# The low part of each query sub-head in a tile of its own, over zeros, in a two-layer diffusion block

## The chip, the core and the metric

The kernel runs on one core of a Trainium2 chip. The metric is the device time of one execution in microseconds (us); three runs of the kernel before took 2702.43, 2704.64 and 2705.81 us, median 2704.64 us. One further execution was profiled, and all rows below are from it. The engines are named as in the profile: PE is the tensor engine's matmul, PEld its weight load, DVE the vector engine, ACT the scalar engine, POOL the GpSimd engine, SP the engine that issues the DMAs.

## The reference

Two layers of a transformer block over 256 context tokens and 512 latent tokens (T = 768), 1024 features wide. A normed and modulated input is projected to four branches: softmax attention A (the differential attention below), attention B (eight heads over latent projections), a pooling mixer and a convolution mixer. They are merged with sigmoid gates, projected, and followed by a squared-relu MLP. Attention A, which the change touches, in the reference's own words:

```
def attend(qs, ks, v, coef):          # qs: (2 sub-heads, batch, 4 heads, tokens, 64)
    ...
        sc = jnp.einsum('mbhqd,mbhkd->mbhqk', qi, ks, preferred_element_type=jnp.float32) * scale
        p = jnp.einsum('m,mbhqk->bhqk', coef, jax.nn.softmax(sc, axis=-1))
        return jnp.einsum('bhqk,bhkd->bhqd', p.astype(v.dtype), v)
```

Each of the four heads has two sub-heads of 64 features; each sub-head has its own scores and its own softmax, and the second is subtracted from the first with a learned weight. In the first layer the 256 context queries see the 256 context keys and the 512 latent queries see all 768 keys; in the second layer only the latent queries are computed.

## The kernel before

All products run in the float32r format. To keep float32 accuracy a value is split into a high part (rounded to float32r by an ACT copy) and a low part (the rest, by a DVE subtraction), and a product is made of high x high, high x low and low x high.

For the scores of attention A the splitting is packed. A sub-head has 64 features, a tile 128 partitions. `a_qk` projects the queries (or keys) of two heads, norms and rotates them token-major, transposes them on the PE into PSUM (`pst`) and writes, for sub-head j of head hd:

- keys: one tile `ks0` or `ks1`, with the high part on the sub-head's own 64 partitions (`me`) and the low part on the other 64 (`other`);
- queries: one tile `qd0` or `qd1`, with the high part on `me` and a full copy of the value on `other`, so that one product over 128 partitions gives high x high plus (value) x low;
- queries, low part: one tile `ql` for both sub-heads, sub-head 0 on partitions 0 to 63 and sub-head 1 on 64 to 127.

`scores` makes a score tile of 128 queries by up to 768 keys in one PSUM buffer (`sc`; its pool has a single buffer): first `qd` x `ks` over 128 partitions, then `ql` x `ks` over the 64 partitions of the sub-head, accumulated. Keys are taken in chunks of 512 and 256 columns, so a tile with 768 keys is four matmuls and one with 256 keys is two. `softmax_exp` takes the maximum on DVE (`st`) and the exponential on ACT (`e`); `a_attn` combines the two sub-heads' tiles, transposes and splits them (`ph`, `pl`), and multiplies with the values `va`. Attention B does the same with 96-feature heads, with separate tiles for high and low (`bqh`, `bql`, `bkh`, `bkl`), always over 96 partitions.

The order of the work is not the order in which the code is written. Every instruction is recorded into streams (B: projections, A: attention, F: filler such as gate, pooling and convolution products, M: modulation vectors); `Plan.order` then gives each a key and lays them out with a model of the engines, and `replay` emits them in that order. Each engine runs its instructions in order. Every instruction is thus recorded at one line, L352, and the profile is read by tiles.

Tiles `ks`, `qd`, `ql`, `va`, `b..`, the split weights `wgh`/`wgl` of the latent projections and the MLP's `ah`/`al` share pool `g`, with 24 buffers of 128 x 768; a new tile waits until a buffer's former tile has been read for the last time. POOL has almost nothing to do: it clears the padding of the pooling and convolution buffers (`pool`, `cu`).

Of the kernel before, what the change touches and what calls it, by code (L numbers as in the profile page):

```python
# [20 lines left out]
# packed per-layer column constants  # L21
C_BM, C_G1, C_G2, C_SP, C_WC, C_GCQ, C_GCKV, C_GS, NCOL = 0, 48, 56, 64, 68, 80, 83, 85, 86
# packed per-layer row constants
# [4 lines left out]
# gate tiles made beside the attention, and the share of that filler at each of its steps, per layer  # L28
# [11 lines left out]
class _Rec:  # L40
    """Stands for an engine while the program is recorded."""
# [10 lines left out]
class Plan:  # L52
    """Orders the recorded instructions over the engines.

    The program is recorded as streams that run side by side within a phase. Every instruction gets a key (how far
    its stream has come, in tensor engine time); a model of the engines then issues, on each engine, the ready
    instruction with the least key. Slots of a pool tag are given out in recorded order."""
# [4 lines left out]
    def __init__(self):  # L62
        self.ops = []        # (eng, fn, meth, args, kw, key)
        self.keys = []
        self.hold = {}       # op -> earliest time
        self.phase = []
        self.nphase = 0
        self.phase_ops = {}
        self.base = 0.0
        self.stream = 'B'  # L70
        self.pe = 0.0
        self.mode = 'ff'

    # ---- recording
# [14 lines left out]
    def flush(self, span=None, lead=None):  # L89
        """ends a phase: streams are spread evenly over the time of the tensor engine in it"""  # L90
        tot = {s: sum(self.ops[i][4] for i in o if self.ops[i][0] == 'PE') for s, o in self.phase_ops.items()}
        all_ = sum(tot.values())
        for s, o in self.phase_ops.items():
            t = 0.0
            eng = 'DVE' if s == 'M' else 'PE'
            f = all_ / max(sum(self.ops[i][4] for i in o if self.ops[i][0] == eng), 1.0)
            off, sc = (lead or {}).get(s, (0.0, 1.0))
            for i in o:
                self.keys[i] = self.base + off * all_ + sc * t * f
                if self.ops[i][0] == eng:  # L100
                    t += self.ops[i][4]
        if HOLD:
            for i in self.phase_ops.get('M', ()):
                if self.ops[i][0] == 'SP':
                    self.hold[i] = self.keys[i] * HOLD
        self.base += all_
        self.phase_ops = {}
        self.nphase += 1
        self.stream = 'B'
# [52 lines left out]
    # ---- ordering  # L162
    def order(self):
# [4 lines left out]
        tiles = {}      # name -> [tag, bufs, first op, number of ops]  # L168
# [40 lines left out]
        # slots  # L209
        tagq, tagfree, first = {}, {}, {}  # L210
        unmet = {}      # tag -> phase -> tiles without a slot yet
# [28 lines left out]
        def try_slots(i):  # L240
            """gives op i the slots of the tiles that it is first to touch, or leaves it waiting"""
            while first.get(i):
                nm_ = first[i][-1]
                tag = tiles[nm_][0]
                if tag.split('_')[0] in self.DYN:
                    ph = self.phase[i]
                    if not tagfree[tag] or any(p < ph for p in unmet[tag]):
                        heapq.heappush(waiting.setdefault(tag, []), (ph, self.keys[i], i))
                        return False
                    t = heapq.heappop(tagfree[tag])  # L250
                    ready_t[i] = max(ready_t[i], t)
                    first[i].pop()
                    unmet[tag][ph] -= 1
                    if not unmet[tag][ph]:
                        del unmet[tag][ph]
                        if tagfree[tag] and waiting.get(tag):
                            wake.append(heapq.heappop(waiting[tag])[2])
                    continue
                q = tagq[tag]
                if q[-1][1] != nm_ or not tagfree[tag]:  # L260
                    return False
                t = heapq.heappop(tagfree[tag])
                ready_t[i] = max(ready_t[i], t)
                q.pop()
                first[i].pop()
                if q and tagfree[tag]:
                    wake.append(q[-1][0])
            return True
# [95 lines left out]
def tile_block(ctx, tc, xT, ccol, wmod, cols, rows, wqkv, wcq, wckv, wuq, wukv, wpool,  # L364
# [61 lines left out]
    def wset():  # L426
        """a weight slot: filler has its own; phases of dense products alone use both sets in turn"""
        if plan.mode != 'attn':
            wturn[0] += 1
            return (wfp, "wf") if wturn[0] % 2 == 0 else (wbp, "wb")  # L430
        return (wfp, "wf") if plan.stream == 'F' else (wbp, "wb")
# [28 lines left out]
    def rsqrt(ss, n, scale):  # L460
        """[128, n] of rsqrt(ss * scale + eps); scale is a float or a list of (lo, hi, scale)."""
# [11 lines left out]
    # ---------------------------------------------------------------- constants  # L473
# [5 lines left out]
    # cosines of all token tiles and sines of the x tiles (context has no rotation), times the gains  # L479
# [13 lines left out]
    # ---------------------------------------------------------------- modulation vectors  # L493
    # silu of c and c_ctx, features on partitions: [128, kt, vector]
# [14 lines left out]
    def mod_half_pe(hf, between=lambda kt: None):  # L509
        """shift and scale of the first norm for half of the features, on the tensor engine"""  # L510
# [19 lines left out]
    def mod_chunk(l, ch):  # L530
        """one chunk of the modulation vectors, products and sums over the feature tiles on the vector
        engine; yields between the feature tiles"""
# [43 lines left out]
    # ---------------------------------------------------------------- feature-major helpers  # L576
# [23 lines left out]
    def norm_r(ss, a, b):  # L600
        """1 / rms of the tokens a..b, on all partitions"""
# [16 lines left out]
    def norm_scale(l, c_g, m0, v, d0, d1):  # L618
        """g * (1 + scale) of the features"""
        ab = st(16)  # L620
        V.scalar_tensor_tensor(out=ab[:, d0:d1], in0=mods[l][:, 8 * (m0 + 1) + d0:8 * (m0 + 1) + d1, v], scalar=1.0,
                               in1=col(l, c_g + d0, d1 - d0), op0=ALU.add, op1=ALU.mult)
        return ab
# [4 lines left out]
    def norm_apply(l, x_t, R, ab, m0, seg, res, d0=0, d1=8, alt=False):  # L628
        """modulate(rmsnorm(x), mod[m0], mod[m0+1]) of a segment as split tiles"""
# [11 lines left out]
    # ---------------------------------------------------------------- layer tables  # L641
# [26 lines left out]
    # ---------------------------------------------------------------- token-major projections  # L668
    def tokmm(ps, off, n, h, w, tt, passes_w):
        """ps[:, off:off+n] = h[tokens tt]^T @ W; w(kt) -> (hi, lo) rhs."""  # L670
        nk = len(h)
        sl = slice(tt * 128, tt * 128 + 128)
        for kt in range(nk):
            hh, hl = h[kt]
            wh, wl = w(kt)
            for i, (a, b) in enumerate(((hh, wh), (hh, wl), (hl, wh))):
                PE.matmul(ps[:, off:off + n], lhsT=a[:, sl], rhs=b, start=(kt == 0 and i == 0),
                          stop=(kt == nk - 1 and i == 2))
# [11 lines left out]
    def a_qk(l, h1, hp, isk, hook):  # L690
        w = ahead.pop() if ahead else chunk_w(l, (2 if isk else 0) + hp)
        res = [tuple(g_tile(n=x) for x in (("ks0", "ks1") if isk else ("qd0", "qd1", "ql"))) for _ in range(2)]
        for tl in halves(l == DEPTH - 1 and not isk):
# [31 lines left out]
            for hd in range(2):  # L725
# [4 lines left out]
                for j in range(2):  # L730
# [5 lines left out]
                    else:  # L736
# [4 lines left out]
                        V.tensor_tensor(out=res[hd][2][me, c], in0=pt[me, :], in1=x[me, c], op=ALU.subtract)  # L741
# [19 lines left out]
    def scores(terms, t, nk):  # L761
        """q tile t with the keys; terms: (q, k, partitions)"""
# [14 lines left out]
    def a_attn(l, q, k, v, head, ydr):  # L777
# [4 lines left out]
        for t in range(t0, 6):  # L782
# [3 lines left out]
            for j in range(2):  # L786
                ps = scores(((q[j], k[j], slice(0, 128)), (q[2], k[j], slice(64 * j, 64 * j + 64))), t, nk)
# [46 lines left out]
    def rope_b_apply(dst, u, n, g, tab, t0, rbuf):  # L834
        """dst, u: [128, n, g, 32] views; tables rows t0.."""
# [11 lines left out]
    def b_latent(l, h1, hook):  # L847
        last = l == DEPTH - 1
        # q latent
# [28 lines left out]
        # kv latent and shared rotary key  # L878
# [147 lines left out]
    # ---------------------------------------------------------------- pool and conv mixers  # L1026
# [4 lines left out]
    def pad_segs(full, a, b):  # L1031
        """(psum/token slice, padded offset) of the segments."""
# [59 lines left out]
    def conv_branch(l, h1, i, ydr):  # L1092
        """yields after each of its three projections"""
# [51 lines left out]
    # ---------------------------------------------------------------- the layers  # L1145
# [27 lines left out]
    for l in range(DEPTH):  # L1173
# [30 lines left out]
        def do_fill():  # L1204
            """emit filler in proportion to the other work of the phase"""
# [11 lines left out]
        # attention inputs and attention  # L1217
# [29 lines left out]
        # gates, branch projections, merge  # L1247
# [45 lines left out]
        # output projection and residual  # L1293
# [10 lines left out]
        def step():  # L1304
            """one feature tile of a norm goes between the products of the other part"""
# [3 lines left out]
        def wkeep(key, src, pi):  # L1309
            """the split weights of a unit; the last units of the first part are used again by the second"""  # L1310
# [23 lines left out]
        # squared-relu MLP  # L1334
# [68 lines left out]
def _prep(i):  # L1403
    """Layouts of the inputs and constants that depend on shapes alone."""
# [77 lines left out]
```

## Time and profile before

| what | value |
|---|---|
| runs of the kernel | 2702.43, 2704.64, 2705.81 us; median 2704.64 us |
| profiled execution: span from the first to the last instruction | 2700.7 us (the page gives no time of it beside the span; the median lies 3.9 us above the span) |
| PE matmul busy | 2671.3 us, 99% of the span, 15620 matmuls |
| PE weight load busy | 2311.1 us, 86% |
| DVE busy | 1753.5 us, 65% |
| ACT busy | 1170.3 us, 43% |
| POOL busy | 3.3 us, 47 instructions |
| granted PE clock, mean | 0.999 of full speed |

The busy time of a matmul in the profile reaches past the moment at which the next one starts, because matmuls are pipelined. What a matmul costs the PE is therefore read from the distance between one start and the next, and these distances stand in the timeline rows.

### The profile page before, as it was taken

Reading aid. Unit: us, or ns where it says so; the run is one execution under the profiler, and the core shown is the slowest. Engines: PE = TensorE matmul, PEld = TensorE weight load, DVE = VectorE, ACT = ScalarE, POOL = GpSimd, SP = SyncE. Lnnn points to the kernel's source line nnn. Section 1 sums busy time; section 2 is a strip of 40 time slices with the busy share of each in tenths; the row PEclk is TensorE's granted clock in tenths of the full one; section 3 lists DMA queues with packets and bytes.
Section 4 is the critical chain, followed back from the end, with each engine's and each line's share of the span. In section 5 each row is a group of like instructions: output and inputs, shape, how many; then the busy total and the mean of one; then the engine's idle time right before and its main releaser. Section 6 shows DMA issues by size and latency. Waiting matters only on the chain.

```text
span 2700.7 us, 41931 instructions
## 1 busy us (share of the span) xinstructions
PE 2671.3 (99%) x15620; PEld 2311.1 (86%) x15620; DVE 1753.5 (65%) x3978; ACT 1170.3 (43%) x2444; POOL 3.3 (0%) x47
## 2 busy tenths in 40 slices
PE   8999999999999999999999999999999999999999
PEld 4888889989998888988888888887888887998887
DVE  6668666689987777445455477776467887743333
ACT  4445443446555235414141444554455562544332
POOL 0000000000000000000000000000000000000000
PEclk9999999999999999999999999999999999999999
DMA  7211223334336743333444422223332366433322
GB/s 243 77 54 58 88 91 116 104 119 129 114 122 203 226 143 104 102 96 107 125 129 129 129 90 85 72 65 99 97 104 71 93 196 213 143 116 94 101 94 78
DMA packets 189533, 311.90 MB, mean 115 GB/s; under 512 B 21520, under 2 KB 72080, under 8 KB 189328
## 3 DMA queue, kind: packets, MB, share of 16 engines
q1 hardware_dynamic: 189328, 309.22, 36.9%
q8 instruction: 123, 2.02, 0.3%
q14 instruction: 82, 0.67, 0.1%
HBM read 270.86 MB, written 38.27 MB: 114 GB/s over the span
## 4 chain that ended last, share of the span: by engine, by line
PE 94%; DMA 2%; DVE 2%; ACT 1%; issue 0%; SPq 0%; ACTq 0%; DVEq 0%
PE mm L352 80%; PE pst L352 8%; PE sc L352 5%; DMA wmp<-in_wmod_dram 1%; DMA tmp<-y 1%; DVE wl L352 0%; ACT wh L352 0%; DMA wr<-in_wff_dram 0%; DMA wr<-in_wqkv_dram 0%; DVE hl L352 0%; DVE e L352 0%; DVE qd L352 0%; PE R L352 0%; DMA gt<-g 0%; DMA y<-yt 0%
## 5 line engine op out<-in xcount | busy, mean ns | idle before, releaser
L352 ACT ACTIVATE wh<-wr 128x512 fp32r<-128x512 f32 (+2 forms) x664 | 396.1, 617 | 738.7 <-PE mm L352 621.6
L352 PE MATMUL mm<-hh,wh 128*128 128x256 f32 (+1 forms) x1984 | 614.7, 354 | 2.2 <-DVE xx L352 1.0
L352 PE MATMUL mm<-hh,wl 128*128 128x256 f32 (+1 forms) x1984 | 613.3, 354 | 0.6 <-DVE wl L352 0.6
L352 PE MATMUL mm<-hl,wh 128*128 128x256 f32 (+1 forms) x1984 | 611.0, 354 | 0.0
L352 DVE TENSOR_TENSOR wl<-wr,wh 128x512 fp32r<-128x512 f32 (+2 forms) x664 | 440.7, 674 | 219.2 <-ACT wh L352 211.1
L352 PEld LDWEIGHTS mm<-hh,wh 128*128 128x128 f32 x1984 | 370.5, 189 | 50.6 <-issue 4.6
L352 PEld LDWEIGHTS mm<-hh,wl 128*128 128x128 f32 x1984 | 371.3, 189 | 49.3 <-issue 3.5
L352 PEld LDWEIGHTS mm<-hl,wh 128*128 128x128 f32 x1984 | 370.8, 189 | 47.7 <-issue 3.0
L352 DVE SCALAR_TENSOR_TENSOR macc<-wm,silu,macc 128x256 f32<-128x256 f32 x448 | 205.2, 479 | 97.5 <-DMA wm<-in_wmod_dram 92.5
L352 PE MATMUL mm<-ah,wh 128*128 128x512 f32 (+1 forms) x768 | 242.0, 355 | 0.4 <-ACT wh L352 0.3
L352 PE MATMUL mm<-al,wh 128*128 128x512 f32 (+1 forms) x768 | 241.8, 355 | 0.0
L352 PE MATMUL mm<-ah,wl 128*128 128x512 f32 (+1 forms) x768 | 241.1, 355 | 0.0
L352 DVE SCALAR_TENSOR_TENSOR xx<-mm,mod,xx 128x256 f32<-128x256 f32 (+1 forms) x96 | 61.3, 659 | 170.2 <-PE mm L352 170.2
L352 ACT ACTIVATE ph<-pst 128x384 fp32r<-128x384 f32 (+1 forms) x216 | 102.9, 477 | 151.6 <-PE pst L352 150.8
L352 PEld LDWEIGHTS mm<-ah,wh 128*128 128x128 f32 x768 | 144.6, 188 | 21.7 <-ACT wh L352 0.8
L352 PEld LDWEIGHTS mm<-al,wh 128*128 128x128 f32 x768 | 144.5, 188 | 20.9 <-issue 0.2
L352 PEld LDWEIGHTS mm<-ah,wl 128*128 128x128 f32 x768 | 144.4, 188 | 20.8 <-issue 0.2
L352 ACT ACTIVATE e<-sc,st 128x768 f32<-128x768 f32 (+1 forms) x160 | 130.2, 814 | 73.5 <-DVE st L352 50.6
L352 PE MATMUL mm<-wl,hh 128*128 128x256 f32 x544 | 156.1, 289 | 0.9 <-DVE wl L352 0.9
L352 PE MATMUL mm<-wh,hh 128*128 128x256 f32 x544 | 155.2, 289 | 1.3 <-ACT wh L352 0.7
L352 PE MATMUL mm<-wh,hl 128*128 128x256 f32 x544 | 154.7, 286 | 0.0
L352 DVE TENSOR_REDUCE st<-sc 128x1 f32<-128x768 f32 (+1 forms) x160 | 135.3, 846 | 23.6 <-PE sc L352 21.5
(195 smaller groups left out, 4570.5 us busy)
## 6 DMA issues: line engine op xcount, KB each, us to landing
wr<-in_wff_dram SPq DMA_DIRECT2D x280, 256.0 KB, 2.9
wr<-in_wdense_dram SPq DMA_DIRECT2D x192, 256.0 KB, 3.0
wm<-in_wmod_dram SPq DMA_DIRECT2D x320, 128.0 KB, 2.2
wr<-in_wbr_dram SPq DMA_DIRECT2D x64, 256.0 KB, 3.7
wr<-in_wqkv_dram SPq DMA_DIRECT2D x48, 256.0 KB, 2.8
g<-gt SPq DMA_DIRECT2D x32, 384.0 KB, 2.6
gt<-g SPq DMA_DIRECT2D x32, 384.0 KB, 3.5
wr<-in_wo_dram SPq DMA_DIRECT2D x48, 256.0 KB, 3.0
```

The source lines that it names most:

```text
L352: ins = fn(*a, **k).ins
```

## The change

Per query sub-head j, the low part gets a tile of its own, `ql0` or `ql1`. It stands on the sub-head's 64 partitions as before; the other 64 partitions are set to zero by a POOL memset. The second score product then uses all 128 partitions of `ql` and of `ks`: the zeros cancel the half of `ks` that holds the keys' low part. Values written and summed are otherwise as before. All other lines of the diff remove comments, which shifts line numbers by six.

```diff
     def a_qk(l, h1, hp, isk, hook):
         w = ahead.pop() if ahead else chunk_w(l, (2 if isk else 0) + hp)
-        res = [tuple(g_tile(n=x) for x in (("ks0", "ks1") if isk else ("qd0", "qd1", "ql"))) for _ in range(2)]
+        res = [tuple(g_tile(n=x) for x in (("ks0", "ks1") if isk else ("qd0", "qd1", "ql0", "ql1"))) for _ in range(2)]
+        if not isk:
+
+            qc = CT if l == DEPTH - 1 else 0
+            for hd in range(2):
+                for j in range(2):
+                    G.memset(res[hd][2 + j][64 - 64 * j:128 - 64 * j, qc:T].bitcast(F32), 0.0)
...
-                        V.tensor_tensor(out=res[hd][2][me, c], in0=pt[me, :], in1=x[me, c], op=ALU.subtract)
+                        V.tensor_tensor(out=res[hd][2 + j][me, c], in0=pt[me, :], in1=x[me, c], op=ALU.subtract)
...
-                ps = scores(((q[j], k[j], slice(0, 128)), (q[2], k[j], slice(64 * j, 64 * j + 64))), t, nk)
+                ps = scores(((q[j], k[j], slice(0, 128)), (q[2 + j], k[j], slice(0, 128))), t, nk)
```

The diff touches a recorded program, so it could move instructions on every engine. On PE, a score tile of the first layer and its neighbours stood like this before (`sc` the score tile, `hh`, `wh`, `wl` the filler's operands; the numbers are counters of names):

```order
L352 MATMUL mm_469<-wl_460,hh_189 128x256
L352 MATMUL mm_469<-wh_459,hl_190 128x256
L352 MATMUL mm_469<-wh_459,hh_191 128x256
L352 MATMUL sc_655<-ks_175_358,qd_110_293 128x512
L352 MATMUL sc_655<-ks_175_358,qd_110_293 128x256
L352 MATMUL sc_655<-ks_175_358,ql_295 128x512
L352 MATMUL sc_655<-ks_175_358,ql_295 128x256
L352 MATMUL mm_469<-wl_460,hh_191 128x256
L352 MATMUL mm_469<-wh_459,hl_192 128x256
```

And the same place on PE in the changed program:

```order
L352 MATMUL mm_473<-wl_462,hh_189 128x256
L352 MATMUL mm_473<-wh_461,hl_190 128x256
L352 MATMUL mm_473<-wh_461,hh_191 128x256
L352 MATMUL sc_659<-ks_177_360,qd_110_293 128x512
L352 MATMUL sc_659<-ks_177_360,qd_110_293 128x256
L352 MATMUL sc_659<-ks_177_360,ql_112_295 128x512
L352 MATMUL sc_659<-ks_177_360,ql_112_295 128x256
L352 MATMUL mm_473<-wl_462,hh_191 128x256
L352 MATMUL mm_473<-wh_461,hl_192 128x256
```

Nothing moved here but the counters in the names. The same holds, apart from those names, for all 15580 matmuls of the program on PE and for every instruction on DVE, ACT and SP. Only POOL differs. At the start of the program's padding work, POOL had before:

```order
masks.py:199 AFFINE_SELECT ident<-ident 128x128
L352 MEMSET pool_376 128x8
L352 MEMSET pool_376 128x16
L352 MEMSET pool_376 128x8
L352 MEMSET pool_431 128x8
L352 MEMSET pool_431 128x16
L352 MEMSET pool_431 128x8
```

And POOL at that place in the changed program, `ql_112` and `ql_113` being the two low tiles of the first head, `ql_116` and `ql_117` those of the second:

```order
masks.py:199 AFFINE_SELECT ident<-ident 128x128
L352 MEMSET ql_112_295 64x768
L352 MEMSET ql_113_296 64x768
L352 MEMSET ql_116_299 64x768
L352 MEMSET ql_117_300 64x768
L352 MEMSET pool_378 128x8
L352 MEMSET pool_378 128x16
L352 MEMSET pool_378 128x8
L352 MEMSET pool_433 128x8
L352 MEMSET pool_433 128x16
L352 MEMSET pool_433 128x8
```

Four memsets came ahead of the padding. There are three more such groups of four: behind `pool_433` in the first layer, and ahead of the first and behind the second padding of the second layer (64 x 512 there); 16 in all. The first score matmul that reads each `ql` tile now also waits for POOL's semaphore, 16 waits in all; no other engine's instruction waits for another engine than before.

## Rows read from the trace of the kernel before

**Rows 1.** The page's head, its busy shares by engine, and the chain that ended last.

```profile
span 2700.7 us, 41931 instructions
PE 2671.3 (99%) x15620; PEld 2311.1 (86%) x15620; DVE 1753.5 (65%) x3978; ACT 1170.3 (43%) x2444; POOL 3.3 (0%) x47
...
PE 94%; DMA 2%; DVE 2%; ACT 1%; issue 0%; SPq 0%; ACTq 0%; DVEq 0%
```

**Rows 2.** Busy by window (stretch, length, PE, PEld, DVE, ACT, POOL, clock, DMA, GB/s).

```profile
130.00:402.00 272.00, 271.58 (x1735) 233.82 (x1734) 186.06 (x442) 132.23 (x317) 0.37 (x6) 1.00 0.24 74
...
1677.00:1895.00 218.00, 217.24 (x1295) 181.56 (x1293) 158.60 (x366) 110.76 (x246) 0.41 (x6) 1.00 0.26 79
```

**Rows 3.** Groups by shape: the low score products (busy, mean ns | idle before).

```profile
L352 PE MATMUL sc<-ks,ql 64*128 64x512 f32 x64 | 31.7, 496 | 0.0
...
L352 PE MATMUL sc<-ks,ql 64*128 64x256 f32 x80 | 23.8, 297 | 0.0
```

**Rows 4.** Timeline, PE (start, us): one 768-key score tile, x2 joining 512 and 256.

```profile
163.50 0.51 PE L352 MATMUL sc<-ks,qd 128*128 128x512 f32 x2
163.94 0.61 PE L352 MATMUL sc<-ks,ql 64*128 64x512 f32 x2
164.49 0.39 PE L352 MATMUL mm<-wh,hl 128*128 128x256 f32 x1
164.71 0.28 PE L352 MATMUL mm<-wh,hh 128*128 128x256 f32 x1
```

**Rows 5.** Timeline, PE: one 256-key score tile and the filler behind it.

```profile
194.64 0.28 PE L352 MATMUL sc<-ks,qd 128*128 128x256 f32 x1
194.84 0.38 PE L352 MATMUL sc<-ks,ql 64*128 64x256 f32 x1
195.16 0.38 PE L352 MATMUL mm<-wl,hh 128*128 128x256 f32 x1
195.38 0.28 PE L352 MATMUL mm<-wh,hl 128*128 128x256 f32 x1
195.50 0.28 PE L352 MATMUL mm<-wh,hh 128*128 128x256 f32 x1
```

**Rows 6.** Timeline, PE: a 768-key tile of attention B, 96 partitions throughout.

```profile
614.21 0.51 PE L352 MATMUL sc<-bkl,bqh 96*128 96x512 f32 x2
614.56 0.53 PE L352 MATMUL sc<-bkh,bql 96*128 96x512 f32 x2
614.92 0.52 PE L352 MATMUL mm<-hl,wh 128*128 128x256 f32 x2
615.28 0.38 PE L352 MATMUL pst<-ident,e 128*128 128x128 f32 x2
```

**Rows 7.** Timeline: exponential and next score tile's weight load, first and last of 79.

```profile
132.03 0.46 ACT L352 ACTIVATE e<-sc,st 128x256 f32<-128x256 f32 x1
...
132.63 0.19 PEld L352 LDWEIGHTS sc<-ks,qd 128*128 128x128 f32 x1
...
1892.59 0.90 ACT L352 ACTIVATE e<-sc,st 128x768 f32<-128x768 f32 x1
...
1894.04 0.30 PEld L352 LDWEIGHTS sc<-ks,qd 128*128 128x128 f32 x2
```

**Rows 8.** Timeline, POOL: the largest memset.

```profile
0.87 0.20 POOL L352 MEMSET ones<- 128x128 f32 x1
```

**Rows 9.** Timeline, second layer: last MLP read of pool g, first use of a cleared padding.

```profile
1598.99 0.28 PE L352 MATMUL mm<-ah,wl 128*128 128x256 f32 x1
...
1620.29 0.71 DVE L352 TENSOR_TENSOR pool<-pool 128x527 f32<-128x527 f32 x1 [0.22 <-ACT pool L352]
```

**Rows 10.** Timeline, first layer: last reads of second and third heads' values, first latent weight.

```profile
271.17 0.28 PE L352 MATMUL pst<-va,pl 128*128 128x256 f32 x1
...
294.15 0.51 ACT L352 ACTIVATE wgh<-wr 128x384 fp32r<-128x384 f32 x1
...
351.48 0.28 PE L352 MATMUL pst<-va,pl 128*128 128x256 f32 x1
```

## The prediction

> **What bounds the kernel now.** I read the page first: in a span of 2700.7 us the PE is busy 99%, and the chain that ended last runs for 94% over the PE [rows 1]. The reader should see that no other engine comes near, DVE at 65%, so microseconds taken from the PE's own stream should reach the end. Then I cut the span into windows to see whether that also holds where the change acts. The scores of attention A lie in 130 to 402 us (first layer) and 1677 to 1895 us (second); there the PE is busy 271.58 of 272.00 us and 217.24 of 218.00 us, DVE 186.06 and 158.60 us, at a granted clock of 1.00, the 2.4 GHz level [rows 2]. A busy PE is not a PE at its best pace, though, so the third view is the timeline, read by the distance from start to start.
>
> **What the low products cost now.** The plain pace is a matmul of 256 columns every 0.12 us (195.38 to 195.50, [rows 5]) and a pair of 512 and 256 columns every 0.35 to 0.36 us [rows 6].
>
> In the 768-key tile the `qd` pair takes 163.94 - 163.50 = 0.44 us, the `ql` pair 164.49 - 163.94 = 0.55 us, and the first filler matmul behind it 0.22 us: 1.21 us for what at the plain pace is 0.35 + 0.35 + 0.12 = 0.82 us. So 0.39 us are lost, 0.09 ahead of the `ql` pair, 0.20 in it, 0.10 behind it [rows 4].
>
> In the 256-key tile the distances are 0.20, 0.32 and 0.22 us against 0.12 each: 0.74 against 0.36, so 0.38 us are lost [rows 5]. The loss is the same for one low matmul as for two: it belongs to the visit, not to the column.
>
> Is it the 64 partitions? The nearest control is attention B, whose products never span 128 partitions but always 96: the `bkl` pair, the `bql` pair behind it, and the 128-partition filler behind that are spaced 0.35, 0.36 and 0.36 us, with no loss going in, inside, or coming out [rows 6]. So neither a partition count below 128 as such, nor a third product into one PSUM tile, nor a change of operands costs anything. What is left that distinguishes `ql` is that it uses half of the array's rows.
>
> The Trainium skill weighs in on both sides here. "TensorEngine Tiling (Array Packing)", section Key Properties, says that changing the tiling mode drains the TensorE, with 64 rows being a mode of its own; by that a visit pays going in and coming out, as the rows show, and the sum would be the one below. "TensorE: Matmul & The Clock Gate", section "Why this matters for your kernels", says that a small contraction takes the same time as a full one, so spanning 128 partitions instead of 64 would change no matmul's time and the sum would be zero; that becomes a rival.
>
> **The change part by part.**
>
> *Removed: the visits.* There are 144 low matmuls, 64 of 512 columns and 80 of 256 [rows 3]. Each 768-key tile has one of each, so 64 visits are of that kind and 80 - 64 = 16 are 256-key tiles. At the plain pace the new products cost what 128-partition products of their columns cost. The gain is 64 x 0.39 + 16 x 0.38 = 31.0 us. Of these, 18.6 fall in the first layer (32 and 16 visits) and 12.5 in the second (32). This is the upper bound of the gain. The lower one is zero, if the loss stays.
>
> *Given back: the score chain.* `sc` has one buffer, so the next score tile waits for the exponential of the last. The part of the loss that lies behind the tile's last start is time in which maximum and exponential run; taking it away brings the PE to the next tile sooner, but not the exponential. From the end of an exponential to the next tile's weight load the first of 79 pairs has 132.63 - (132.03 + 0.46) = 0.14 us and the last 1894.04 - (1892.59 + 0.90) = 0.55 us [rows 7]. 0.14 is the shortest of all 79 and occurs twelve times, so I take it as the hop itself: there the PE already waits. How much of the loss lies behind the tile's last start is between 0.10 us (the filler's share in [rows 4]) and 0.20 + 0.10 = 0.30 us (in [rows 5], where the visit has one low matmul, less its 0.08 ahead). I take half of the 0.39, 0.19 us. Then a gap shorter than 0.14 + 0.19 = 0.33 us turns into a wait; 33 of the 79 are, and what they lack adds up to 4.6 us. A wait at one tile loosens the next, so this is rather too much than too little; I keep it whole for what other short waits appear. Net: 31.0 - 4.6 = 26.4 us.
>
> *Added: 16 memsets on POOL*, 64 x 768 (eight) and 64 x 512 (eight). The trace has none of that size; the largest, 128 columns, takes 0.20 us [rows 8]. In proportion that is at most 6 x 0.20 = 1.2 us and 0.8 us, 16 us together; the lower bound, a fixed 0.20 each, is 3 us. They cost nothing as long as POOL's 3.3 us of work [rows 1] are not late. Behind the memsets in POOL's queue stand the paddings of the pooling buffers, and DVE waits for these. The tightest place is the start of the second layer: the four tiles need buffers that the MLP last reads at 1598.99 us, the padding behind them is first read by DVE at 1620.29 us, and four memsets need at most 3.2 us of these 21 [rows 9]. If DVE were held while POOL writes, 16 us of a DVE idle for a third of the time would be hidden too: I take nothing, and keep 2 us for the range.
>
> *Added: four more tiles per layer in pool `g`.* The two head pairs now want 32 buffers out of 24 instead of 28, so tiles behind them wait for earlier releases. The keys and values of the second pair (eight) now take exactly the first head's eight; the eight latent weights need the second head's, last read at 271.17 us and wanted from 294.15 us [rows 10]: 23 us to spare. That cover hides it.
>
> *Added: 16 waits of score matmuls for POOL.* Each is for a memset done long before; nothing.
>
> *Not moved:* PE, DVE, ACT and SP keep their order, so no DMA is issued past another.
>
> **Sum.** In the profiled execution, 2700.7 - 26.4 = 2674.3 us of span; the median of the runs lies 3.9 us above the span, and I carry that over: 2704.6 - 26.4 = **2678 us**.
>
> **The rivals.**
>
> *The score chain takes back all that lies outside the tile.* If DVE and ACT, asked to keep up with a faster PE, set the pace at every tile, only what is lost inside a tile is gained: about 0.20 of the 0.39 us in 64 visits and 0.08 in 16, together 14 us: 2691 us. For it: the gaps are short, 33 of 79 under 0.33 us. Against it: the other 46 are longer, and DVE and ACT are busy 68% and 49% of the first layer's window [rows 2].
>
> *The change does not do what it says.* If the loss belongs to the packed accumulation and not to the 64 partitions, the visit costs what it did: 2704.6 us. For it: the rule on small contractions named above. Against it: attention B accumulates three products over 96 partitions without loss [rows 6].
>
> *Slower: pool `g`.* If the four extra tiles push the latent weights to the third head's release, they come at 351.48 instead of 294.15 us, up to 57 us later [rows 10]. It decides only where filler no longer fills the PE and the idle time exceeds the 26 us gained; in the worst case 57 - 26 = 31 us remain: up to 2736 us. Against it: the spare 23 us, and the unchanged order on all four engines.
>
> **How the numbers follow.** The forecast has 0.77, its own range 2672 (the full 31.0 with a little more) to 2685 us (twice the 4.6 us given back, and the 2 us of POOL). The chain rival has 0.13 at 2691, no change 0.05 at 2705, slower 0.04 up to 2736; 0.01 is left for something faster still. The range runs from 2671 to 2691, the chain rival's time, and leaves out at most 0.15. A measurement of this kernel can tell about 0.2%, 5.4 us, from no change: faster 0.91, same 0.05, slower 0.04.
>
> **What would show each step right or wrong.** In the changed timeline a `ql` pair should be followed 0.35 us later by filler, and that by its successor 0.12 us later; `qd` to `ql` should shrink from 0.44 to 0.35 us. If these distances stay, the second rival holds. If they shrink, but the weight load of the next `qd` stands 0.14 us behind the exponential at most of the 79 places and the two windows shorten by less than 15 us together, the first rival holds. PE idle time ahead of the latent projections, or POOL rows that end late, would speak for pool `g`. The prediction fails if the PE gets new waits of more than some 10 us in the two windows, or if the loss sits elsewhere than in these visits.

## The result, and the profile after

The changed kernel takes 2676.41 us, median of four runs (2674.15 to 2676.63); the kernel before, on the same chip, 2703.68 us (2702.43 to 2705.81, four runs). The ratio is 0.9898, 95% interval [0.9884, 0.9912]: 27.3 us faster. The forecast was 2678 us, 26.4 us faster. The profiled execution has a span of 2674.9 us, 25.8 us less than [rows 1]; 2674.3 had been worked out for it.

The page after, head, busy shares and the chain that ended last:

```profile
span 2674.9 us, 41960 instructions
PE 2643.3 (99%) x15620; PEld 2310.8 (86%) x15620; DVE 1754.0 (66%) x3978; ACT 1172.6 (44%) x2444; POOL 13.4 (1%) x63
...
PE 92%; DVE 3%; DMA 3%; ACT 1%; issue 1%; SPq 0%; DVEq 0%; ACTq 0%
```

Against [rows 1], the PE's busy time fell by 28.0 us with the same 15620 matmuls, DVE and ACT hardly changed, and POOL gained 10.1 us for its 16 memsets. The span fell by 2.2 us less than the PE's busy time. Tile by tile, the 15620 matmuls of the two profiles (not 15580, as the section on the change has it) stand in the same order, so every distance before has its counterpart after.

The two visits that the prediction was worked out from, in the timeline of PE after (start, duration in us):

```profile
162.79 0.52 PE L352 MATMUL sc<-ks,qd 128*128 128x512 f32 x2
163.14 0.53 PE L352 MATMUL sc<-ks,ql 128*128 128x512 f32 x2
163.50 0.28 PE L352 MATMUL mm<-wh,hl 128*128 128x256 f32 x1
163.62 0.28 PE L352 MATMUL mm<-wh,hh 128*128 128x256 f32 x1
...
191.27 0.28 PE L352 MATMUL sc<-ks,qd 128*128 128x256 f32 x1
191.39 0.28 PE L352 MATMUL sc<-ks,ql 128*128 128x256 f32 x1
191.51 0.28 PE L352 MATMUL mm<-wl,hh 128*128 128x256 f32 x1
191.63 0.28 PE L352 MATMUL mm<-wh,hl 128*128 128x256 f32 x1
```

Read the starts: the 768-key tile goes 0.35, 0.36, 0.12 us where [rows 4] went 0.44, 0.55, 0.22; the 256-key tile 0.12 three times where [rows 5] went 0.20, 0.32, 0.22. Every distance is at the plain pace; in these two visits the 0.39 us are gone whole.

The weight loads of the first tile show what form the loss had. The loads of the `ql` pair and of the filler behind it, before (in brackets the idle time ahead of the load, which nothing in the profile explains):

```profile
163.94 0.29 PEld L352 LDWEIGHTS sc<-ks,ql 64*128 64x128 f32 x2 [0.25 <-issue]
...
164.48 0.19 PEld L352 LDWEIGHTS mm<-wh,hl 128*128 128x128 f32 x1 [0.25 <-issue]
```

and after, with the group of the 512-column `ql` matmuls (busy, mean ns) to set beside [rows 3]:

```profile
163.02 0.31 PEld L352 LDWEIGHTS sc<-ks,ql 128*128 128x128 f32 x2
...
163.38 0.19 PEld L352 LDWEIGHTS mm<-wh,hl 128*128 128x128 f32 x1
...
L352 PE MATMUL sc<-ks,ql 128*128 128x512 f32 x64 | 25.3, 395 | 0.0
```

After, both loads start 0.12 us ahead of their own matmul, under the one before it. Before, going to 64 partitions and coming back, each load starts together with its matmul (163.94 and 164.49 us, [rows 4]). What holds it back inside the PE no row shows.

Where the time came from is seen at the first matmul of a tile, the same one in both kernels. The last tile of the first layer and the first and last of the second, after:

```profile
385.95 0.59 PE L352 MATMUL sc<-ks,qd 128*128 128x512 f32 x2
...
1662.54 0.55 PE L352 MATMUL sc<-ks,qd 128*128 128x512 f32 x2
...
1870.59 0.59 PE L352 MATMUL sc<-ks,qd 128*128 128x512 f32 x2
```

and before:

```profile
401.19 0.59 PE L352 MATMUL sc<-ks,qd 128*128 128x512 f32 x2
...
1676.13 0.51 PE L352 MATMUL sc<-ks,qd 128*128 128x512 f32 x2
...
1894.06 0.60 PE L352 MATMUL sc<-ks,qd 128*128 128x512 f32 x2
```

So 15.2 us were gained up to the last tile of the first layer's attention A, 1.6 us were lost again up to the first tile of the second layer's, 9.9 us were gained from there to its last tile, and 2.3 us behind that. A visit's loss lies behind the start of its tile, so the first stretch holds 47 visits and the third 31; they had been priced at 18.2 and 12.1 us, of which 2.9 and 2.2 us were not kept. Of the last 2.3 us, 0.4 are the last visit. The rest cannot be put down to the scores: in the merge of the second layer the PE of the kernel before waited for DVE (`mm<-yh,wh`, 1.45 and 0.80 us, ending at 2244 and 2254 us) where after it waited 0.48 us once, and the run with the additions alone (below), which gains nothing, is 2.3 us shorter in this stretch as well.

### The profile page after: what moved, and what is told of

Same layout as the page of the kernel before. It is cut to its first block, busy times and chain, and to the rows that moved or that the text cites. A ratio compares the mean times of both kernels' runs of the same rounds, so it can differ in the third digit from the quotient of the medians.

```text
span 2674.9 us, 41960 instructions
## 1 busy us (share of the span) xinstructions
PE 2643.3 (99%) x15620; PEld 2310.8 (86%) x15620; DVE 1754.0 (66%) x3978; ACT 1172.6 (44%) x2444; POOL 13.4 (1%) x63
## 4 chain that ended last, share of the span: by engine, by line
PE 92%; DVE 3%; DMA 3%; ACT 1%; issue 1%; SPq 0%; DVEq 0%; ACTq 0%
PE mm L352 79%; PE pst L352 8%; PE sc L352 4%; DMA wmp<-in_wmod_dram 1%; DMA tmp<-y 1%; ACT wh L352 0%; DVE wl L352 0%; DMA wr<-in_wqkv_dram 0%; DVE hl L352 0%; DVE e L352 0%; DMA wm<-in_wmod_dram 0%; DVE ks L352 0%; DVE qd L352 0%; DVE st L352 0%; PE R L352 0%
```

## The experiments

Two theories were set against each other. *Rows*: the loss is paid whenever the PE goes from products that use the full height of the array to one that uses half of it, and back. *Packing*: it belongs to how attention A is built, the shared `ql` tile or the accumulation of a second kind of product into the tile. A third question was whether the additions cost something, and a fourth where the rest of the 31 us went.

**One sub-head only.** The `scores` call of the changed kernel, with sub-head 1 back at 64 partitions:

```diff
-  (q[2 + j], k[j], slice(0, 128))
+  (q[2 + j], k[j], slice(0, 128) if j == 0 else slice(64, 128))
```

> The changed kernel, but only sub-head 0's low product spans 128 partitions; sub-head 1's reads its 64 partitions as before. Tiles, memsets and orders are those of the changed kernel. If the loss is paid per visit to half of the rows, 40 of the 80 visits remain: half of 31.0 us gained, less half of what the score chain takes back, some 13 us, about 2690 us. If the gain came from giving each sub-head its own low tile, nothing is lost: 2676 us.

Measured: 2687.29 us (2686.54 to 2689.56), ratio to before 0.9940 [0.9924, 0.9957], 15.3 us faster, against a kernel before of 2702.57 us here. A little over half of 27.3 us. Both sub-heads had a tile of their own, so the tile is not what gains; the visits are, one by one.

**The additions alone.** All tiles and memsets of the changed kernel, products as before:

```diff
-  (q[2 + j], k[j], slice(0, 128))
+  (q[2 + j], k[j], slice(64 * j, 64 * j + 64))
```

> The changed kernel with all of its tiles and memsets, but both low products read 64 partitions again. If the loss is paid per visit and the additions cost nothing, the time is that of the kernel before within 2 us, 2702 to 2706. If separate tiles bring the gain, 2676. If the 16 memsets and four more tiles per layer cost something that the gain hid, above 2706.

Measured: 2702.40 us (2700.69 to 2706.28, ten runs), ratio 0.9997 [0.9988, 1.0007]. The 16 memsets, the eight more tiles and the changed release of buffers cost nothing that 25 runs of the kernel before against ten can tell. In the changed kernel's timeline of POOL the memsets look like this (start, duration of the group):

```profile
1.46 2.31 POOL L352 MEMSET ql<- 64x768 f32 x3
8.46 0.73 POOL L352 MEMSET ql<- 64x768 f32 x1 [4.70 <-PE mm L352]
...
101.94 3.10 POOL L352 MEMSET ql<- 64x768 f32 x4
...
1326.76 2.25 POOL L352 MEMSET ql<- 64x512 f32 x4 [743.22 <-PE mm L352]
...
1639.63 2.25 POOL L352 MEMSET ql<- 64x512 f32 x4
```

A memset of 64 x 768 takes 0.77 us and one of 64 x 512 takes 0.56 us, inside the bounds of 0.2 and 1.2 us that [rows 8] gave. All are done over 100 us before a score matmul reads their tiles. The four at 1326.76 us show that the tightest place had been misjudged on the safe side: free buffers were there long before the MLP's last read in [rows 9].

**The loss carried elsewhere.** In the changed kernel, attention B's third product cut to 64 and to 32 partitions:

```diff
-  scores([(a, b, slice(0, 96)) for a, b in ((q[0], k[0]), (q[0], k[1]), (q[1], k[0]))], ...)
+  scores([(a, b, pp) for a, b, pp in ((q[0], k[0], slice(0, 96)), (q[0], k[1], slice(0, 96)), (q[1], k[0], slice(0, 64)))], ...)
```

> The changed kernel, with attention B's third score product (low query part) cut from 96 to 64 partitions, which leaves 32 features out of that product. Its 80 score tiles are as many and as wide as attention A's. If going to 64 rows and back costs 0.39 us wherever it stands, 31 us come back, less what waits of attention B absorb: 2702 to 2708. If the loss belonged to attention A's packing, 2676.

Measured: 2709.03 us (2706.10 to 2711.49, ten runs), ratio to before 1.0023 [1.0013, 1.0032], 32.6 us above the changed kernel's median in the first comparison and 1 us past the expected range. The expectation counted 80 visits, one for each tile, but the trace has 91: in 11 of the 768-key tiles full-height products stand between the two low matmuls, as here (timeline of PE):

```profile
630.38 0.49 PE L352 MATMUL sc<-bkh,bql 64*128 64x512 f32 x1
630.81 0.44 PE L352 MATMUL pst<-ident,e 128*128 128x128 f32 x2
631.18 0.38 PE L352 MATMUL sc<-bkh,bql 64*128 64x256 f32 x1
631.49 0.31 PE L352 MATMUL pst<-ident,tmp 128*96 128x128 f32 x1
```

Set against the changed kernel's trace, matmul by matmul, the 91 visits are 33.2 us longer, 0.38 us at the median.

> As the run with 64 partitions in attention B, but 32 (64 features left out of that product). If any row count that makes a smaller tile of the array pays the same change of mode, 2702 to 2708 again. If only 64 does, 2676. If each halving adds its own loss, above 2715.

Measured: 2708.13 us (2704.90 to 2710.94, ten runs), ratio to before 1.0016 [1.0007, 1.0026], 31.7 us above; its 91 visits are 33.1 us longer, again 0.38 us at the median. One tile of this run, timeline of PE:

```profile
602.63 0.51 PE L352 MATMUL sc<-bkh,bqh 96*128 96x512 f32 x2
602.98 0.51 PE L352 MATMUL sc<-bkl,bqh 96*128 96x512 f32 x2
603.42 0.61 PE L352 MATMUL sc<-bkh,bql 32*128 32x512 f32 x2
603.96 0.39 PE L352 MATMUL mm<-wh,ckvh 128*128 128x256 f32 x1
604.19 0.28 PE L352 MATMUL mm<-wl,ckvh 128*128 128x256 f32 x1
```

The distances are 0.35, 0.44, 0.54 and 0.23 us. The first is the plain pace from one 96-partition pair to the next; the other three are [rows 4] over again, with 32 partitions in place of 64 and in another attention. Packing falls. So does the idea that less height means more loss: 32 partitions pay what 64 pay, 96 pay nothing.

**Twice as many changes.** The kernel before with the loops of `scores` swapped, and the changed kernel with the same swap:

```diff
-        for i, (a, b, pr) in enumerate(terms):
-            for c0, c1 in ((0, min(nk, 512)), (512, nk)):
+        for c0, c1 in ((0, min(nk, 512)), (512, nk)):
+            for i, (a, b, pr) in enumerate(terms):
```

> The kernel before with the loops of the score function swapped: per chunk of keys the 128-partition product and then the low one, so that a 768-key tile of attention A goes to 64 partitions twice, with the same matmuls. If the loss is paid per change of the row count, 64 visits are added at 0.39 us: 25 us more, less what the score chain absorbs, 2722 to 2729. If the loss belongs to the tile or to the number of low matmuls, 2704.

Measured: 2729.10 us (2727.61 to 2730.30), ratio 1.0097 [1.0081, 1.0112], 27.2 us slower than the kernel before, 2701.86 us in this comparison; the interval, 22 to 30 us, takes in the 25 us of the price. A tile of it, timeline of PE:

```profile
165.31 0.39 PE L352 MATMUL sc<-ks,qd 128*128 128x512 f32 x1
165.64 0.49 PE L352 MATMUL sc<-ks,ql 64*128 64x512 f32 x1
166.06 0.38 PE L352 MATMUL sc<-ks,qd 128*128 128x256 f32 x1
166.37 0.38 PE L352 MATMUL sc<-ks,ql 64*128 64x256 f32 x1
166.68 0.39 PE L352 MATMUL mm<-wh,hl 128*128 128x256 f32 x1
166.91 0.28 PE L352 MATMUL mm<-wh,hh 128*128 128x256 f32 x1
```

From 165.31 to 166.91 are 1.60 us, for the same columns that take 0.82 at the plain pace: 0.78 us lost, twice 0.39. The matmuls and their operands are the same, and in attention A's windows nothing else changed places: only the number of changes between 128 and 64 doubled. In attention B, whose tiles the swap reaches too, the ordering also laid out other products differently; the next run has the very same order of all 15620 matmuls and is the control for that.

> The changed kernel with the same swap of loops. All products span 128 partitions (96 in attention B), so the swap should cost nothing by either theory: 2674 to 2679. It shows what the swap itself does, apart from the partitions.

Measured: 2675.10 us (2674.24 to 2678.26), ratio to before 0.9901 [0.9888, 0.9915], the changed kernel's own time. The swap itself costs nothing. Between the two swapped kernels lie 54.0 us for 144 visits, and matmul by matmul these visits differ by 54.8 us, 0.38 us each.

**Where the rest went.** Both kernels with a shorter chain from scores to the next score tile:

```diff
-  V.tensor_reduce(s_[:, i:i + 1], ps[:, :nk], axis=AX.X, op=ALU.max, negate=True)
+  V.tensor_reduce(s_[:, i:i + 1], ps[:, 0:nk:m or 1], axis=AX.X, op=ALU.max, negate=True)
...
-  S.activation(e[:, :nk], ps[:, :nk], AF.Exp, ...)
+  S.activation(e[:, :nk], ps[:, :nk], AF.Tanh if m else AF.Exp, ...)
```

Here m is 4 for the 768-key tiles of attention A, 1 for its 256-key tiles, and none for attention B; the ordering model is charged for the full width.

> The kernel before with a shorter score chain in attention A: for 768-key tiles the maximum is taken over every fourth score, and a tanh stands in place of the exponential, so the softmax of attention A is left out; the order of all engines is unchanged. Some 0.5 us are taken from each of 64 maxima. If the score chain makes the PE wait at the few tiles with the shortest gaps only, this gains at most 1 to 2 us: 2701 to 2704. If the chain sets the pace at most tiles, it gains over 5 us.

Measured: 2702.10 us (2699.59 to 2706.04, eleven runs), ratio 0.9999 [0.9990, 1.0008]: no change to within 3 us, so this chain did not set the pace of the kernel before.

> The changed kernel with the same shorter score chain and the same softmax left out. If what was not gained (31.0 us expected of the visits, some 27 measured) went into waits for the exponential, the distance to the kernel before with the short chain is 29 to 31 us. If it is 26 to 27 us again, the visits were worth less than 31 us, or the waits are for something else.

Measured: 2673.94 us (2671.28 to 2676.66), ratio to before 0.9895 [0.9881, 0.9908]. That is 28.2 us from the short-chain kernel before, between the two expectations, and the intervals, some 3 us to either side, take in both. The group of maxima in its profile shows that the edit did shorten the chain, from 0.95 to 0.35 us each (all 32 + 64 + 64 tiles of both attentions; attention A's 64 are the 192-column ones):

```profile
L352 DVE TENSOR_REDUCE st<-sc 128x1 f32<-128x768 f32 x64 | 61.0, 953 | 12.0 <-PE sc L352 11.4
L352 DVE TENSOR_REDUCE st<-sc 128x1 f32<-128x192 f32 x64 | 22.6, 353 | 4.2 <-PE sc L352 2.8
```

The waits of the weight loads in the first layer's window say more. Kernel before, 130 to 402 us (total, times, longest):

```profile
PEld sc L352 <- issue: 9.2, 37, 0.3
PEld mm L352 <- issue: 8.1, 32, 0.4
PEld sc L352 <- ACT e L352: 0.5, 2, 0.4
```

Changed kernel, 130 to 387 us:

```profile
PEld sc L352 <- ACT e L352: 1.6, 4, 0.7
PEld pst L352 <- PE sc L352: 0.8, 2, 0.4
PEld sc L352 <- DVE ks L352: 0.6, 1, 0.6
```

Changed kernel with the short chain, 130 to 387 us:

```profile
PEld sc L352 <- ACT e L352: 1.7, 4, 0.7
PEld sc L352 <- DVE ks L352: 0.8, 1, 0.8
PEld pst L352 <- PE sc L352: 0.8, 2, 0.4
```

The waits put down to nothing ("issue") stand where the height changes: 17.3 us here before, 9.4 us with one sub-head only, 0.4 us in the changed kernel. New waits came, but small ones, 1.1 us more for the exponential and 1.2 us for two other things, and shortening the maximum by 0.6 us left them as they were. In the second layer's window (1663 to 1871 us) the 0.7 us that the changed kernel's weight loads wait for the exponential are gone with the short chain.

## Why the prediction was right

**The gain per visit** was the main step, and it held: the loss of 0.38 to 0.39 us a visit is gone from the timeline after, about halved with half of the visits, doubled in a tile with two, and carried to attention B at 0.38 us a visit. Matmul by matmul, the 80 visits became 29.5 us shorter, where 31.0 had been forecast: most by 0.38 or 0.39 us, six by about 0.3, and two of the 256-key tiles by nothing, because a transpose just behind them now waits for DVE's key tiles. That it is a matter of the rows used was argued from attention B's 96 partitions alone [rows 6]; the run with 32 partitions and the swapped loops show it.

**What is given back** was right in its sum and only partly in its mechanism; that the sum came out so close is in part luck. Of 31.0 us, 5.2 are missing in the profiled execution and 3.7 in the medians; 4.6 had been put down. But the forecast said that 33 of the 79 gaps between an exponential and the next score tile's weight load would close. Paired as in [rows 7], 17 gaps stand at the shortest value, 0.14 us, after, where 12 stood before, and the median gap fell from 0.43 to 0.32 us, by 0.1 and not by 0.19: too large a share of the loss had been placed behind the tile. The weight loads' waits for the exponential grew by 1.6 us in both windows together, and a chain shorter by 0.6 us won back part of that, in the second layer.

Where the rest went, the two traces show when distance is set against distance. Of the 5.2 us, 1.5 are missing in the visits themselves. Another 3.1 us were lost between the visits of the two windows: 1.1 of them in four waits for the exponential, the only item that the 4.6 us had been worked out from, and 0.9 in one wait for DVE's key tiles and one for the ACT copy of a filler weight; the others are each about 0.2 or less. Everything outside the two windows adds up to 0.5 us lost. Two runs that take as long as the kernel before, the additions alone and its short chain, differ from it by up to 0.8 us in one window and by up to 2.3 us in a stretch outside, so the smaller items have no cause that could be named.

**The additions** were put at nothing, and cost nothing: 0.9997 with all of them and no gain. The place named as tightest was not tight at all, since the memsets found free buffers some 260 us ahead of the MLP's last read, 1584.7 us in that trace.

**The rivals.** The score chain as the pace-maker at every tile (2691 us) is out with the result, and so is no change. The short chain agrees with the first: the kernel before does not feel it, and the changed kernel by 0.9 us in its distance to the kernel before and 2.5 us in the medians, no more than the noise. The Trainium skill's rule on small contractions ("TensorE: Matmul & The Clock Gate", "Why this matters for your kernels") does not carry over to a product that stands among full-height ones: a 512-column `ql` matmul took 496 ns over 64 partitions [rows 3] and 395 ns over 128, and a visit 0.39 us less. It speaks of a single matmul, and no run here has one by itself. The Trainium skill's rule on changes of the tiling mode ("TensorEngine Tiling (Array Packing)", Key Properties) agrees with every run as to when the price is paid, and the runs put a number to it, 0.38 to 0.39 us for going in and coming out; that the engine drains meanwhile, no row shows. Pool `g` did not bind: with the additional tiles and without the gain, the time is that of the kernel before.

## What to carry to other kernels

In this kernel, a product over 64 or 32 partitions that stands alone among full-height products costs the PE about 0.39 us per visit beyond its columns, at 256 as at 512 and 256 columns; padding its operand with zeros to the full height cost no PE time. Look for it in the distances from start to start, since a PE that is busy 99% hides it, and price it per change of height, not per matmul or per tile: count the visits in the trace, as the ordering can split a tile's visit in two. Then look at what waits one step behind: what the PE gains behind a product that another engine is waiting for is not all kept.

## What was not expected of the hardware

The price did not depend on the height: 32 partitions cost what 64 cost (31.7 and 32.6 us for 91 visits), and 96 cost nothing [rows 6]. Nor did it depend on the number of narrow matmuls in a visit: one of 256 columns [rows 5] and a pair of 512 and 256 [rows 4] lose 0.38 and 0.39 us. And the swap of two loops, which changes neither a matmul nor an operand, moved the kernel before by 27 us and the changed one not at all.
